# Second layer's mixer in periods of two heads with a written TensorE order: a two-layer trunk on one Trainium2 core

## The chip, the core and the metric

The kernel runs on one core of one Trainium2 chip. The time is the device time of one execution in microseconds (us), as the median of several runs. The engines are named as the profile names them: PE is TensorE's matmul stream and PEld its weight loads, DVE is VectorE, ACT is ScalarE, POOL is GpSimd, SP is the queue that issues the DMAs. PSUM is the accumulator memory that PE writes: 8 banks, each 512 fp32 values wide on 128 partitions.

A matmul of type fp32r leaves one record in the trace. A plain fp32 product leaves two, so that "x14" at the value products of the mixer stands for seven instructions; a transpose leaves one.

## The reference, cut to what matters

The program is a trunk of two layers over 512 tokens of width 1024. Each layer has a token mixer and a sparse mixture of experts; layer 0 mixes by a differential attention, layer 1 by stick-breaking attention. Only the second mixer is rewritten by the change:

```python
def stick_breaking_attention(h, w_in, w_out):
    """A[t,s] = sig(z_ts) * prod_{s<j<t} (1 - sig(z_tj)), s < t."""
    q, k, v = jnp.split(h @ w_in, 3, axis=-1)        # 16 heads of 64
    for i in range(S // Q_BLOCK):                    # 4 query blocks of 128
        q0, q1 = i * Q_BLOCK, (i + 1) * Q_BLOCK
        z = jnp.einsum('bqhd,bkhd->bhqk', q[:, q0:q1], k[:, :q1]) * scale
        log_fail = jnp.where(strict, jax.nn.log_sigmoid(-z), 0.0)
        between = lax.cumsum(log_fail, axis=-1, reverse=True) - log_fail
        a = jnp.where(strict, jnp.exp(jax.nn.log_sigmoid(z) + between), 0.0)
        outs.append(jnp.einsum('bhqk,bkhd->bqhd', a, v[:, :q1]))
    return jnp.concatenate(outs, axis=1).reshape(B, S, D) @ w_out

for i in range(DEPTH):       # h: normed, shifted and scaled by rows of cond @ ada_w[i]
    x = x + gate_1 * mixer_i(h)
    x = x + gate_2 * hierarchical_moe(h2)   # router: top-1 group, top-2 of its 8 experts
```

## The kernel before

**Arithmetic.** Activations lie transposed in SBUF, split into a high and a low fp32r part (`R_HI`, `R_LO`). Every weight piece is split likewise by `split_weights`: ACT copies the high part (L470), DVE subtracts for the low part (L471), each in two halves of 128x1024. The split pieces use two pairs of buffers in turn. A product is then three fp32r matmuls (high·high, high·low, low·high).

**Layer 1's mixer.** It runs over four groups of four heads. `qkv` makes the columns of q and k (L496 to L498, 96 matmuls of 512 columns per group) and the values (L511 to L513, 96 matmuls of 256 columns); k is brought out of PSUM by DVE (L502). `stick_group` then takes the group's two pairs of heads, and of each pair the four query blocks from the shortest (128 keys) to the longest (512 keys). For one block:

1. PE: scores of both heads (L591, fp32, 64 rows of the array each).
2. ACT: sigmoid of both heads at once (L594); POOL: causal mask by an affine select (L596); POOL: 1 − sigmoid (L599) into a second buffer, and a memset of one column (L601).
3. DVE: a scan from the last key to the first for each head (L605) into a third buffer, then the product with the sigmoid (L606).
4. PE: transposes of the 128x128 blocks (L611) into the only bank `tp`; ACT: copies out (L617).
5. PE: value products, one per block of keys and head, 128 columns each (L621); after four query blocks ACT copies the pair's result out (L624).

**What sets the order.** The PSUM tiles come from a pool by name: `mm` (2 banks), `sc` (2 times 2 banks), `tp` (1), `o` (1). The order of the instructions on each engine is set by a scheduler from the code; it puts matmuls of the next group's `qkv`, and at the end of the output product, between the scores, transposes and value products of a pair. In layer 1, chunks of the conditioning matrix (ada) for later are folded in beside it: DVE sums them in halves of 128x1024 (L322, the first of a set L319), PE turns the sum into a row (L331).

**After the mixer** the transposed result is split in eight blocks (L1185 on ACT, L1186 on DVE). `out_proj` multiplies by the output weights in two halves of columns (n = 0 and n = 1; L665 to L667, 24 matmuls for each tile of 128 tokens), adds to x with the gate (L686, L688), transposes (L692) and makes the router's logits (L699); at n = 1 the logits of n = 0 are added by L697, and routing of the tile follows, mostly on DVE. `router_prepare` makes the router's bias row (L635, L638, L640). Then the experts run (first matmul of each L1072, second L1087); their weights come through SP's queue into free slots of SBUF, in order, as slots come free (L124).

## Time and profile before

| | us |
|---|---|
| time, median of 3 runs (1639.03 to 1640.78) | 1640.48 |
| the profiled execution | 1638.01 |
| its span on the core | 1636.3 |
| PE busy | 1563.1 (96%) |
| DVE busy | 832.1 (51%) |
| ACT busy | 439.0 (27%) |
| POOL busy | 65.1 (4%) |

The span is the time from the first to the last instruction of the profiled execution. Stages overlap at their edges; the trace puts them at these times:

| stage (us from the start of the span) | from | to |
|---|---|---|
| layer 1: value products of the first group's `qkv` begin | 812.5 | |
| layer 1: first scores; last value products of the mixer | 850.0 | 1081.3 |
| layer 1: first logits of n = 1 (routing begins) | 1104.9 | |
| layer 1: first expert matmul | 1148.9 | |
| end of the span | | 1636.3 |

The busy time of an engine is a share over all stages; the start of a record and the start of the next one on the same engine tell how long it holds the engine, since the matmuls are pipelined and their records overlap.

### The profile page before, as it was taken

The numbers are of one execution on the slowest core, as the hardware profiler recorded it, in microseconds if no ns is written. First come the engines' busy times: TensorE is split into PE (matmuls) and PEld (weight loads), VectorE is DVE, ScalarE is ACT, GpSimd is POOL, SyncE is SP. The second block draws the span as 40 slices with busy tenths as digits, with TensorE's granted clock in tenths as the row PEclk, the third lists the DMA queues.
The fourth block names the chain that finished last, engine by engine and source line by source line (L and its number), as shares of the span: only waits on it lengthen the run. The fifth ranks groups of instructions, "written<-read, shape, count | busy, mean of one in ns | idle before, by whom it ended". The sixth has DMA issues, their size and how long they took to land. (4 is left out here: it accounts for less than half of the span.)

```text
span 1636.3 us, 20917 instructions
## 1 busy us (share of the span) xinstructions
PE 1563.1 (96%) x8205; PEld 920.4 (56%) x8205; DVE 832.1 (51%) x1777; ACT 439.0 (27%) x835; POOL 65.1 (4%) x120
## 2 busy tenths in 40 slices
PE   5999999899999999999799999998999999999996
PEld 2787778735454454554576675677354444544543
DVE  5888665743344244233676665547543343442435
ACT  4456555321111110110443333344211011111102
POOL 0000000000000000000003212210000000000000
PEclk9999999899999999999899999999999999999998
DMA  9886443199999999999863361331899999999994
GB/s 381 316 293 198 144 143 129 52 362 422 420 421 421 421 420 421 421 421 413 300 245 111 129 209 52 102 128 40 334 420 421 421 421 420 422 420 421 421 415 189
DMA packets 111521, 501.65 MB, mean 307 GB/s; under 512 B 14832, under 2 KB 39440, under 8 KB 65336
## 3 DMA queue, kind: packets, MB, share of 16 engines
q1 hardware_dynamic: 109688, 498.01, 76.9%
q10 hardware_dynamic: 1728, 2.23, 0.5%
q8 instruction: 68, 1.11, 0.3%
q14 instruction: 37, 0.30, 0.1%
HBM read 495.97 MB, written 4.23 MB: 306 GB/s over the span
## 5 line engine op out<-in xcount | busy, mean ns | idle before, releaser
L1072 PE MATMUL sc<-slots 128*64 128x512 f32 x2048 | 460.9, 594 | 2.7 <-DMA slots<-in_expert_w_up_dram 2.7
L1072 PEld LDWEIGHTS sc<-slots 128*64 128x64 f32 x2048 | 155.7, 137 | 301.6 <-issue 279.8
L1087 PE MATMUL sc<-slots 128*64 128x512 f32 x1024 | 226.8, 595 | 2.0 <-ACT slots L904 1.7
L895 DVE TENSOR_TENSOR slots<-slots,sc 128x512 f32<-128x512 f32 x32 | 22.0, 687 | 279.2 <-ACT slots L894 279.2
L1087 PEld LDWEIGHTS sc<-slots 128*64 128x64 f32 x1024 | 71.5, 137 | 137.1 <-issue 130.9
L908 DVE SCALAR_TENSOR_TENSOR slots<-sc,slotw,slots 128x512 f32<-128x512 f32 x64 | 45.1, 747 | 186.9 <-PE sc L1087 186.9
L927 PE MATMUL mm<-rslots 128*128 128x512 f32 x512 | 131.9, 410 | 7.4 <-DMA slots<-in_sb_w_in_dram 4.4
L927 PEld LDWEIGHTS mm<-rslots 128*128 128x128 f32 x512 | 97.2, 195 | 42.8 <-issue 21.9
L894 ACT ACTIVATE slots<-sc 128x512 f32<-128x512 f32 x32 | 19.2, 599 | 373.6 <-PE sc L1072 373.6
L917 ACT ACTIVATE rslots<-slots 128x512 fp32r<-128x512 f32 x64 | 39.9, 631 | 292.4 <-DVE slots L908 291.1
L1040 PEld LDWEIGHTS mm<-hot,rslots 128*128 128x128 f32 x896 | 109.1, 191 | 11.4 <-issue 11.4
L1040 PE MATMUL mm<-hot,rslots 128*128 128x256 f32 x896 | 114.4, 286 | 0.0
L930 DVE TENSOR_TENSOR slots<-mm,slots 128x512 f32<-128x512 f32 x144 | 95.6, 686 | 31.7 <-PE mm L927 30.0
L496 PE MATMUL mm<-rslots 128*128 128x512 f32 x256 | 104.7, 410 | 4.2 <-ACT rslots L433 3.7
L497 PE MATMUL mm<-rslots 128*128 128x512 f32 x256 | 103.9, 406 | 0.3 <-DVE rslots L434 0.3
L498 PE MATMUL mm<-rslots 128*128 128x512 f32 x256 | 104.0, 406 | 0.0
L471 DVE TENSOR_TENSOR rslots<-slots,rslots 128x1024 fp32r<-128x1024 f32 x64 | 77.9, 1228 | 44.1 <-ACT rslots L470 44.0
L322 DVE SCALAR_TENSOR_TENSOR slots<-slots,consts 128x1024 f32<-128x1024 f32 x70 | 88.6, 1290 | 6.3 <-DMA slots<-in_ada_w_dram 6.3
L470 ACT ACTIVATE rslots<-slots 128x1024 fp32r<-128x1024 f32 x64 | 66.6, 1054 | 74.2 <-PE mm L497 53.0
L511 PE MATMUL mm<-rslots 128*128 128x256 f32 x256 | 72.5, 284 | 1.5 <-ACT rslots L458 1.5
L513 PE MATMUL mm<-rslots 128*128 128x256 f32 x256 | 72.6, 284 | 0.2 <-DVE rslots L459 0.2
L512 PE MATMUL mm<-rslots 128*128 128x256 f32 x256 | 72.6, 284 | 0.0
(243 smaller groups left out, 2020.5 us busy)
## 6 DMA issues: line engine op xcount, KB each, us to landing
slots<-in_expert_w_gate_dram SPq DMA_DIRECT2D x104, 1024.0 KB, 18.8
slots<-in_expert_w_up_dram SPq DMA_DIRECT2D x104, 1024.0 KB, 15.2
slots<-in_expert_w_down_dram SPq DMA_DIRECT2D x104, 1024.0 KB, 15.7
slots<-in_ada_w_dram SPq DMA_DIRECT2D x48, 1024.0 KB, 7.4
slots<-in_expert_w_gate_dram SPq DMA_DIRECT2D x48, 512.0 KB, 6.2
slots<-in_expert_w_up_dram SPq DMA_DIRECT2D x48, 512.0 KB, 6.6
slots<-in_expert_w_down_dram SPq DMA_DIRECT2D x48, 512.0 KB, 9.1
slots<-in_diff_w_in_dram SPq DMA_DIRECT2D x12, 1024.0 KB, 5.2
```

What stands on the lines that cost most here:

```text
L322: add = dve.scalar_tensor_tensor(acc[:, c_], sl(s)[:, c_], cs[:, kb:kb + 1], acc[:, c_], op0=ALU.mult, op1=ALU.add)
L471: j = dve.tensor_tensor(rs_(ls)[:, cs_], sl(s)[:, cs_], rs_(hs)[:, cs_].bitcast(F32), op=ALU.subtract)
L496: pe.matmul(pt, lhsT=wh[:, kb, cc], rhs=rT(R_HI, kb), start=(kb == 0), stop=False)
L497: pe.matmul(pt, lhsT=wh[:, kb, cc], rhs=rT(R_LO, kb), start=False, stop=False)
L498: pe.matmul(pt, lhsT=wl[:, kb, cc], rhs=rT(R_HI, kb), start=False, stop=(kb == KB - 1))
L512: pe.matmul(po, lhsT=rT(R_HI, kb, ts), rhs=wl[:, kb, :], start=False, stop=False)
L513: pe.matmul(po, lhsT=rT(R_LO, kb, ts), rhs=wh[:, kb, :], start=False, stop=(kb == KB - 1))
L927: chain(pe.matmul(pt, lhsT=sT[:, P * i:P * i + P], rhs=parts[nn][part], start=(n + part == 0), stop=(n == len(group) - 1 and part == 1)))
L930: dve.tensor_tensor(xn, pt, xn, op=ALU.add)
L1040: chain(pe.matmul(pt[:, 256 * kk:256 * kk + 256], lhsT=rT(r, kb, slice(P * i, P * i + P)), rhs=sb[:, i, :], start=(i == 0 and r == R_HI), ...
L1072: chain(pe.matmul(pg[64 * e:64 * e + 64, w, :], lhsT=hTe[:, kb, c0:c0 + 64], rhs=sl(ws[e])[:, 512 * kk:512 * kk + 512], start=(kb == 0), s ...
L1087: chain(pe.matmul(pd[64 * e:64 * e + 64, nn, :], lhsT=hidT[:, fb, 64 * e:64 * e + 64], rhs=sl(ws[e])[:, c0:c0 + 512], start=(fb == 0), sto ...
```

## The change

**PSUM.** The pool's tiles are replaced by one tile `banks` of 8 banks; `mm`, `sc`, `tp` and `o` become fixed views of banks 0–1, 2–5, 6 and 7.

**Line.** `qkv` is cut into units: a unit of columns is 24 matmuls (one q or k block of 128 columns), a unit of values 48. `Line` holds the queue of units and splits the weights of two pieces ahead. In layer 0 six units are run before each group's mixer. In layer 1 every PE instruction of the mixer is linked to the one before it (`chain`), so that the written order holds on PE.

**Stick.** One class for the mixer of layer 1. In period n (n = 0 to 7, a pair of heads each) the order is: scores of query blocks 3 and 2; value products of pair n − 1; one unit; scores of query blocks 1 and 0; one unit; transposes of the upper blocks (14); one unit; transposes of the lower blocks (6). After the columns of a group are used up, the ten units of the output product's first half stand in the queue (`first_out`).

- 1 − sigmoid is computed by ACT as the sigmoid of the negated score (L659), so ACT does 64 sigmoids instead of 32, POOL does 64 affine selects instead of 32 and none of the 32 of L599. The last column of ones is set once.
- The scan runs in place (L674); the mask and the product stay (L675).
- Value products take two query blocks at once: 12 matmuls per pair, of 256 or 128 columns (L713), instead of 20 of 128 (the same 1280 columns for each head).
- Copies out of PSUM: two of 128x896 on ACT for the upper blocks (L699), one of 128x384 on ACT (L690) and one each of 128x256 and 128x128 on DVE (L687, L688) for the lower ones. k of layer 1 is copied by ACT.
- The bank of the second head's lower transposes is that of the pair's value result (bank 7).
- ada chunks in layer 1 are summed at two points of each period (`ada_later`), not when they are met in the queue.

**Out of order before.** `router_prepare` stands in period 6; the splits of blocks 0 to 5 in period 6, of 6 in period 7, of 7 after the last value products. x is loaded in period 7. The transposes of n = 0 use banks 4 and 5 in turn.

```diff
@@ the score step, the scan and the value products @@
-                act.activation(sg[:, :, 0:kl], pt[:, :, 0:kl], AF.Sigmoid)
...
-                pool.tensor_scalar(fb[:, :, 0:kl], sg[:, :, 0:kl], -1.0, 1.0, op0=ALU.mult, op1=ALU.add)
...
-                    dve.tensor_tensor_scan(dst, src, src, 1.0, op0=ALU.mult, op1=ALU.bypass)
...
+                act.activation(fx[:, :, at:at + kl - 1], pt[:, :, p0 + 1:p0 + kl], AF.Sigmoid, scale=-1.0)
...
+                act.activation(sg[:, :, at:at + kl], pt[:, :, p0:p0 + kl], AF.Sigmoid)
...
+                    f = fx[:, hh, at:at + kl - 1][:, ::-1]
+                    dve.tensor_tensor_scan(f, f, f, 1.0, op0=ALU.mult, op1=ALU.bypass)
...
-                for kb in range(qb + 1):
-                    for hh in range(2):
-                        pe.matmul(po[64 * hh:64 * hh + 64, P * qb:P * qb + P],
...
+            for kb, t0, aT, start, stop in steps:
+                for hh in range(2):
+                    hs = slice(64 * hh, 64 * hh + 64)
+                    chain(pe.matmul(po[hs, t0:t0 + aT[hh].shape[-1]], lhsT=v[:, kb, P * c + 64 * hh:P * c + 64 * hh + 64],
+                                    rhs=aT[hh], start=start, stop=stop))
@@ the body of layer 1 @@
-        for g in range(4):
-            q, k, v = qkv(l, g, qkv_sl, first if g == 0 else None)
-            mix(g, q, k, v, xo_sl, *rings)
...
+            line.run(4)
+            for n in range(8):
+                stick.scores(n, 0)
+                ada_later()
+                if n:
+                    stick.values(n - 1)
...
+                line.run(2 if n == 7 else 1)
...
+                stick.scores(n, 1)
+                ada_later()
+                line.run()
+                stick.transposes(0)
...
+                if n < 7:
+                    line.run()
+                stick.transposes(1, (4, 5) if n == 7 else (6, 7))
+            line.run()
+            stick.values(7)
+            split_block(xo_sl, 7)
+            line.run()
```

PE in the first group, before: scores, transposes and value products of one query block stand in between single matmuls of the next group's columns.

```order
L591 MATMUL sc<-slots 128x384
L621 MATMUL o<-slots 64x128 x5
L591 MATMUL sc<-slots 128x384
L611 MATMUL tp<-consts,slots 128x128 x4
L496 MATMUL mm<-rslots 128x512
L497 MATMUL mm<-rslots 128x512
L498 MATMUL mm<-rslots 128x512
L496 MATMUL mm<-rslots 128x512
L611 MATMUL tp<-consts,slots 128x128 x4
L621 MATMUL o<-slots 64x128
L497 MATMUL mm<-rslots 128x512
```

PE at the border of period 0 and period 1 in the changed kernel: L529 and L530 end a unit of columns, L684 are the lower transposes, L655 scores, L713 value products.

```order
L529 MATMUL banks<-rslots 128x512
L530 MATMUL banks<-rslots 128x512
L684 MATMUL banks<-consts,slots 128x128 x6
L655 MATMUL banks<-slots 128x512 x2
L655 MATMUL banks<-slots 128x384 x2
L713 MATMUL banks<-slots 64x256 x4
L713 MATMUL banks<-slots 64x128 x2
L713 MATMUL banks<-slots 64x256 x4
L713 MATMUL banks<-slots 64x128 x2
L528 MATMUL banks<-rslots 128x512
L529 MATMUL banks<-rslots 128x512
```

The score products of both heads and the value products of a whole pair now stand together, and the columns' matmuls in blocks of 24.

DVE in the second group, before: for each query block two scans and a product, with splits of weights (L471) and copies of k (L502) between them.

```order
L605 SCALAR_TENSOR_TENSOR slots<-slots 128x255 x2
L606 TENSOR_TENSOR slots<-slots 128x2x256
L605 SCALAR_TENSOR_TENSOR slots<-slots 128x383 x2
L471 TENSOR_TENSOR rslots<-slots,rslots 128x1024
L606 TENSOR_TENSOR slots<-slots 128x2x384
L605 SCALAR_TENSOR_TENSOR slots<-slots 128x511 x2
L471 TENSOR_TENSOR rslots<-slots,rslots 128x1024
L606 TENSOR_TENSOR slots<-slots 128x1024
L502 COPY slots<-mm 128x512
```

DVE at the border of period 1 and period 2 in the changed kernel: the lower scans, the splits of the next weights (L474), the copies of the lower transposes (L687, L688), the upper scans of the next pair.

```order
L674 SCALAR_TENSOR_TENSOR slots<-slots 128x255 x2
L674 SCALAR_TENSOR_TENSOR slots<-slots 128x127
L675 TENSOR_TENSOR slots<-slots 128x2x256
L674 SCALAR_TENSOR_TENSOR slots<-slots 128x127
L675 TENSOR_TENSOR slots<-slots 128x2x128
L474 TENSOR_TENSOR rslots<-slots,rslots 128x1024 x3
L687 COPY slots<-banks 128x256
L688 COPY slots<-banks 128x128
L474 TENSOR_TENSOR rslots<-slots,rslots 128x1024
L674 SCALAR_TENSOR_TENSOR slots<-slots 128x511 x2
L675 TENSOR_TENSOR slots<-slots 128x2x512
```

Two of the copies out of PSUM now stand on DVE, behind three half splits, where ACT alone did them before.

PE at the last value products, before, with the output product's matmuls (L665 to L667) around them:

```order
L611 MATMUL tp<-consts,slots 128x128 x4
L621 MATMUL o<-slots 64x128
L667 MATMUL sc<-rslots 128x512
L665 MATMUL sc<-rslots 128x512
L666 MATMUL sc<-rslots 128x512
L621 MATMUL o<-slots 64x128 x7
L667 MATMUL sc<-rslots 128x512
```

PE at the same place in the changed kernel (L742 to L744 are the output product):

```order
L744 MATMUL banks<-rslots 128x512
L713 MATMUL banks<-slots 64x256 x4
L713 MATMUL banks<-slots 64x128 x2
L713 MATMUL banks<-slots 64x256 x4
L713 MATMUL banks<-slots 64x128 x2
L742 MATMUL banks<-rslots 128x512
```

Of the 120 matmuls of the output product that come before the routing of the first tile (L697 before, L796 after), 44 stand ahead of the last value products before the change; in the changed kernel it is 75.

## Rows read from the trace of the kernel before

**Rows 1.** Windows: stretch, length, busy time of each engine, clock, DMA share, GB/s.

```profile
812.50:1081.00 268.50, 255.38 (x1493) 181.16 (x1494) 167.38 (x200) 101.08 (x174) 60.31 (x97) 0.99 0.42 144
...
1300.00:1320.00 20.00, 20.00 (x124) 12.00 (x122) 3.94 (x8) 3.38 (x6) 0.00 (x0) 1.00 1.01 422
```

**Rows 2.** Timeline of SP's queue ahead of layer 1's experts: start, length.

```profile
1099.13 52.76 SPq L124 DMA_DIRECT2D slots<-in_expert_w_down_dram  x7
```

**Rows 3.** Timeline of PE at both ends of the stretch and at the experts' start.

```profile
812.50 0.38 PE L511 MATMUL mm<-rslots 128*128 128x256 f32 x1 [1.51 <-ACT rslots L458]
...
1104.86 0.31 PE L697 MATMUL o<-logits,consts 128*128 128x40 f32 x2
...
1148.94 5.61 PE L1072 MATMUL sc<-slots 128*64 128x512 f32 x22
```

**Rows 4.** Timeline of PE: matmuls whose starts give what each kind holds.

```profile
818.20 0.28 PE L512 MATMUL mm<-rslots 128*128 128x256 f32 x1
818.32 0.28 PE L513 MATMUL mm<-rslots 128*128 128x256 f32 x1
...
849.49 0.39 PE L497 MATMUL mm<-rslots 128*128 128x512 f32 x1
849.72 0.39 PE L498 MATMUL mm<-rslots 128*128 128x512 f32 x1
850.04 0.93 PE L591 MATMUL sc<-slots 64*128 64x128 f32 x8
...
853.02 1.77 PE L591 MATMUL sc<-slots 64*128 64x384 f32 x8
857.30 0.33 PE L611 MATMUL tp<-consts,slots 128*128 128x128 f32 x1 [2.51 <-DVE slots L606]
...
892.17 0.60 PE L611 MATMUL tp<-consts,slots 128*128 128x128 f32 x4
892.70 0.43 PE L621 MATMUL o<-slots 128*64 128x128 f32 x2
...
893.95 1.09 PE L621 MATMUL o<-slots 128*64 128x128 f32 x14
894.97 0.50 PE L496 MATMUL mm<-rslots 128*128 128x512 f32 x1
```

**Rows 5.** Groups of 812 to 1105, PE only: busy, mean ns, idle before.

```profile
L699 PE MATMUL o<-wra,slots 128*128 128x40 f32 x32 | 4.1, 277 | 0.0
...
L640 PE MATMUL o<-rrow,ones_r 1*128 1x40 f32 x2 | 0.4, 288 | 0.0
```

**Rows 6.** Groups of 812 to 1082, shapes apart, columns as in Rows 5.

```profile
L322 DVE SCALAR_TENSOR_TENSOR slots<-slots,consts 128x1024 f32<-128x1024 f32 x28 | 36.0, 1302 | 0.0
L471 DVE TENSOR_TENSOR rslots<-slots,rslots 128x1024 fp32r<-128x1024 f32 x27 | 33.2, 1236 | 32.3 <-ACT rslots L470 32.3
...
L596 POOL TENSOR_SCALAR_AFFINE_SELECT slots<-slots 128x256 f32<-128x256 f32 x32 | 20.7, 647 | 163.7 <-ACT slots L594 157.5 <-DVE slots L605 3.7 <-DVE slots L322 2.5
...
L605 DVE TENSOR_TENSOR_SCAN slots<-slots 128x511 f32<-128x511 f32 x16 | 18.7, 1207 | 6.6 <-POOL slots L599 6.6
L605 DVE TENSOR_TENSOR_SCAN slots<-slots 128x383 f32<-128x383 f32 x16 | 14.4, 942 | 12.8 <-POOL slots L599 12.8
...
L606 DVE TENSOR_TENSOR slots<-slots 128x1024 f32<-128x1024 f32 x8 | 10.2, 1269 | 0.5
L606 DVE TENSOR_TENSOR slots<-slots 128x768 f32<-128x768 f32 x8 | 9.6, 1206 | 0.5
...
L594 ACT ACTIVATE slots<-sc 128x1024 f32<-128x1024 f32 x8 | 8.2, 1020 | 0.0
```

**Rows 7.** Windows of layer 1's norm and of the first scores, columns as in Rows 1.

```profile
790.00:800.00 10.00, 5.58 (x21) 3.07 (x18) 4.16 (x6) 4.43 (x5) 0.00 (x0) 0.77 0.78 276
...
850.00:860.00 10.00, 6.99 (x35) 3.81 (x34) 9.21 (x12) 4.39 (x7) 3.14 (x5) 1.00 0.61 206
```

**Rows 8.** Timeline of DVE and PE in layer 0's mixer.

```profile
70.02 2.49 DVE L322 SCALAR_TENSOR_TENSOR slots<-slots,consts 128x1024 f32<-128x1024 f32 x2
...
76.99 1.04 PE L331 MATMUL mm<-slots,ones_r 128*32 128x512 f32 x2
```

More of the change, by code (lines that the diff above doesn't have):

```diff
@@ L74, in trunk_kernel @@
     loaded = deque()
+    later = deque()
     state = {"reserve": 0}
@@ L105, in fetch, with ada_later @@
                 return s
+            later.append((s, ada))
+            if not state.get("lazy"):
+                ada_later()
+    def ada_later():
+        while later:
+            s, ada = later.popleft()
             ada_step(s, *ada)
@@ L480, in rT, with __init__, split, add @@
         return rs_(ss[kb // 4])[:, 512 * (kb % 4) + tok.start:512 * (kb % 4) + tok.stop]
-    def qkv(l, g, qkv_sl, first=None):
+    class Line:
+        def __init__(self, units, holds):
+            self.units, self.todo, self.holds = deque(), deque(), holds
+            self.left, self.w, self.open = {}, {}, 0
+            for key, unit in units:
+                self.add(key, unit)
+        def split(self, n=2):
+            while self.todo and self.open < n:
+                key = self.todo.popleft()
+                self.w[key] = split_weights(fetch(), self.holds.get(key))
+                self.open += 1
+        def add(self, key, unit):
+            if key not in self.left:
+                self.left[key] = 0
+                self.todo.append(key)
+            self.left[key] += 1
+            self.units.append((key, unit))
+        def run(self, n=1):
+            for _ in range(n):
+                self.split()
+                key, unit = self.units.popleft()
+                unit(*self.w[key])
+                self.left[key] -= 1
+                self.open -= not self.left[key]
+    def qkv_views(qkv_sl, g):
         half = slice(1024 * (g % 2), 1024 * (g % 2) + 1024)
@@ L656, in out_proj @@
         )
+        tp0 = Ring([banks[:, b, :].rearrange("p (k t) -> p k t", k=4) for b in (4, 5)])
         for n in range(2):
[L658 to L667 removed]
+            if n or not pts:
+                hl = [split_weights(fetch()) for _ in range(2)]
             if n == 1:
@@ L671, in out_proj @@
                 st["acc"] = [sc_ps(), sc_ps()]
-            else:
-                two = sc_ps()
-                pts = [mm_ps(), mm_ps(), two[:, 0, :], two[:, 1, :]]
+            elif not pts:
+                pts = [mm_ps(), mm_ps(), banks[:, 2, :], banks[:, 3, :]]
                 for i in range(NT):
-                    product(i, pts[i], 0)
+                    out_piece(pts[i], i, range(4), *hl[0])
+                rest = [lambda i=i: out_piece(pts[i], i, range(4, KB), *hl[1]) for i in range(NT)]
             for i in range(NT):
@@ L741, in route_tile @@
         pe.matmul(pr, lhsT=ident, rhs=base, start=True, stop=False)
-        pe.matmul(pr, lhsT=upper, rhs=both, start=False, stop=True)
+        ranked = pe.matmul(pr, lhsT=upper, rhs=both, start=False, stop=True)
         pos = small.tile([P, NE], F32, name="pos")
@@ L762, in route_tile @@
         if i < NT - 1:
-            pc = o_ps()[:, 0:NE]
-            pe.matmul(pc, lhsT=ones, rhs=both, start=True, stop=True)
+            pc = o_ps()[:, 128:128 + NE]
+            behind(pe.matmul(pc, lhsT=ones, rhs=both, start=True, stop=True), ranked)
             st["base"] = small.tile([P, NE], F32, name="base")
@@ L1159, in trunk_kernel @@
             reserve(4)
-        first = split_weights(fetch(), (None, diags[1]) if l else None)
+        qkv_sl = alloc(3)
+        acc_sl.extend(alloc(1))
+        reserve(0)
+        units = []
+        for g in range(4):
+            parts = part_order(l, g)
+            if l == 0:
+                order = [(part, n) for part in parts for n in range(2)]
+            elif g == 0:
+                order = ((2, 0), (2, 1), (0, 0), (1, 0), (0, 1), (1, 1))
+            else:
+                order = ((0, 0), (1, 0), (0, 1), (1, 1), (2, 0), (2, 1))
+            units.append((g, order))
+        linked.clear()
+        link = chain if l else lambda inst: inst
+        holds = {(0, 2): (None, diags[1]), (0, 0): anchor} if l else {}
+        line = Line([u for g, order in units for u in qkv_units(l, g, qkv_sl, order, link)], holds)
+        line.split(1)
         if l == 0:
```

279 lines of the change are left out of this document (177 added, 102 removed).

## Prediction, made before the changed kernel was run

> **What bounds the kernel now.** I read the windows first. In layer 1's experts PE is busy all the time and the DMA engines are full as well, at 422 GB/s [rows 1]. The second question is when this phase begins. SP's queue stands still for 52.76 us before it [rows 2]: the free slots have been filled, and the queue waits for PE to give back the first of them. So the weight stream does not set the start of the phase; PE's arrival sets the start of the stream, and the phase moves as a whole with the first expert matmul at 1148.94 [rows 3]. Before that come 44.1 us of routing from the first logits of n = 1 at 1104.86 [rows 3], which the change leaves as they are. What is left is the stretch from the first value products of `qkv` at 812.50 to 1104.86, 292.4 us. In its main part PE is busy 255.4 of 268.5 us at a clock of 0.99, DVE 167.4, ACT 101.1, POOL 60.3 [rows 1]. PE bounds it, with only 13.1 us of idle time. A change that only hid waits could win no more than these. The larger part must come from PE's own time: how long its instructions hold it.
>
> **What each kind holds.** I take the distance from start to start [rows 4]. A value product of `qkv`: 0.12 us. A product of 512 columns (columns of q and k, output product): 0.23. The last of a run before fp32 work holds 0.32, so a change of kind costs about 0.1. The scores of 384 and 512 keys of both heads stand together in one place, 7 blocks of 128 keys in 1.77 us: 0.25 per block for both heads, and 0.21 if the last matmul's own length (about 0.3) is taken off. Transposes: 0.53 us for four up to the next kind, 0.13 each, or 0.11 without the change of kind. Value products of the mixer, in the longest run there is: seven instructions, that is 3.5 blocks for both heads, in 1.02 us, 0.29 per block. Two heads side by side, as the scores show it, would give 0.21.
>
> **The sum of PE's work in the changed kernel**, same stretch:
> - value products of `qkv`: 384 × 0.12 = 46.1
> - columns of q and k: 384 × 0.23 = 88.3
> - output product, 96 of n = 0 and 24 of n = 1: 120 × 0.23 = 27.6
> - scores: 8 pairs × 10 blocks × 0.25 = 20.0 (bounds 17 and 20)
> - value products: the same 80 blocks. Pieces of 256 columns are not in the trace. I take 0.23, nearer to the scores (both are plain fp32 with the heads side by side, and all 12 stand together): 18.4 (bounds 17 and 23)
> - transposes: 160 × 0.11 = 17.2 (up to 20.8)
> - norm, ada, router and logit products, unchanged: seven groups from L699 with 4.1 to L640 with 0.4 [rows 5], together 15.9
> - changes of kind: per period three excursions into fp32 (scores with values, short scores, upper transposes; the lower ones run on into the next scores), each twice 0.1: 8 × 3 × 0.2 = 4.8
>
> Together 238.3 us. Against 292.4 that is 54.1 less: 13.1 is the idle time, and 41 is what mixing single matmuls of different kinds costs now.
>
> **What the order on PE makes of the waits.** PE now goes through a written order, so what is not ready stops all that is behind it: the next unit, and with it the copies that ACT and DVE wait to make. I follow the chain of the upper blocks. After the scores ACT needs 1.0 us for the first sigmoid, POOL 0.65 for the mask, DVE 2 × 1.21 + 1.27 + 2 × 0.94 + 1.21 = 6.8 for scans and products [rows 6]: 8.5 us. That scans in place take as long as now I assume; no row shows it. Before PE comes to the upper transposes it has the values (2.3), the short scores (0.75) and two units (2 × 5.5): 14.1 us. So 5.6 us are spare, and DVE can have four halves of split or ada ahead (1.24 and 1.30 each [rows 6]). The lower chain is shorter and has a unit and the upper transposes as cover. ACT's 32 added sigmoids cost at most 1.0 each [rows 6], 33 us over 230: ACT stays at some 60% and covers them. POOL trades 32 copies for 32 selects.
>
> The spare time goes in some places. (1) The second head's lower transposes lie in bank 7, which the value products of the same pair overwrite after 1.75 us of scores. Between them stand DVE's two copies, behind up to three half splits. If DVE is in the middle of such a half, PE waits: about 0.8 us after periods 1, 3 and 5, and 1.7 after period 2, where four ada halves stand ahead; 4.1 in all. (2) In period 6 the router's bias row needs DVE's sum, which stands behind the upper chain: 5.5 us of unit against 8.5 of chain, 3 us. (3) The transposed ada row in period 4: 1.5. Together 8.6 us (estimate; 2 if DVE meets them all early, 14 if each is doubled). 292.4 − 238.3 − 8.6 = **45.5 us** won.
>
> **Layer 0.** Its code only gets new names and fixed banks, but its order shifts: the first ada row of PE comes about 7 us earlier. DVE's sum for it ends at 72.5, PE took it at 76.99 [rows 8], so PE now waits up to 2.5 us, and at the next one perhaps 1. I take 2 (0 to 6, since a fixed ring of banks could also cost elsewhere).
>
> **The number.** 1638.0 (profiled execution) − 45.5 + 2 = 1594.5. The median of the runs is 2.5 above the profiled execution: **1597 us**. With the low bounds (values and scores 17, waits 2, switches 3, layer 0 none) it is 1582; with the high ones (values 23, transposes 20.8, waits 14, layer 0 plus 6) 1615.
>
> **Rivals.**
> A. The chain on DVE is the bound. In period 2 DVE has more to do than PE: upper chain 6.8, lower 3.5, eleven ada halves 14.3, two splits 2.5, copies 0.7, together 27.8 against about 25 of PE. Where ada and splits stand ahead of the scans in all periods, as in the first three, the wait is about 2.5 us each: 8 × 2.5 = 20 less won, 1617 us. For it speaks that the order on DVE is fixed too; against it that the later periods carry no ada sums and DVE is at 62% now.
> B. Slower than before, by the clock. In the norm of layer 1 PE was busy 5.58 of 10 us and the granted clock was 0.77 [rows 7]. If the new waits fall into every period and bring the mean granted clock over the mixer to about 0.80 (parts of it at the lower level of 1.2 GHz instead of 2.4), its 238.3 us become 298, and with 8.6 of waits and layer 0's 2 the stretch is 16 us longer than now: 1657 us. It decides from a clock of about 0.85 on, where what was won is used up. Against it: a wait of 2.51 us before 857.30 [rows 4] lies in a window with clock 1.00 [rows 7], and I expect none longer than 3. The Trainium skill (TensorE: Matmul & The Clock Gate, HAM oscillation) says that a kernel whose bursts of matmuls are parted by waits can swing between the two clock levels; it speaks against any order that makes PE wait, and this trace shows it in the norm and not in the mixer.
> C. The mixer is shorter and the end does not move, since the experts stream their weights at the DMA limit. Then the time is 1640. Against it stands the queue that waits 52.76 us for a slot [rows 2]; for it only that DMA share is 1.01 afterwards [rows 1].
> D. The change of kind is not cheaper: the 41 us of mixing are really the cost of reading fp32 operands, and the longer blocks bring back only half, 20 us, beside the idle time less the new waits (4.5). Then 1640.5 − 24.5 + 2 = 1618. Against it: 0.23 in undisturbed runs and 0.32 at a change are both in the rows. The Trainium skill (TensorEngine Tiling (Array Packing), Key Properties) says that a change of the tiling mode drains the array. By that rule only the borders of the mixer's 64-row and 64-column products would cost, and the transposes among the columns would be free; the sum would then be 1 to 2 us lower, at the same forecast.
>
> **How the numbers follow.** Forecast 0.72, A 0.12, B 0.03, C 0.03, D 0.10. Forecast and the two partial ones lie from 1582 to 1618; I take 1582 to 1619, which leaves out B and C and the tails. A measurement of this kernel can tell 0.2%, 3.3 us, from no change. Faster 0.94, same 0.03, slower 0.03.
>
> **What would show it.** In the changed trace: first routing logits about 1061 instead of 1104.86, then again 44 us to the first expert matmul; columns at 0.23 in blocks of 24; a pair's value products in 2.1 to 2.9 us; PE's waits in the mixer under 14 us, most at the value products (for DVE's copies) and the router row; clock at 0.99 there; SP's queue still waiting before the experts. If PE waits at the upper transposes in most periods, A is right; if the clock is below 0.9 in the mixer, B; if the experts' first matmul moves and the end does not, C; if the waits are small and the blocks are no faster, D.

## The result and the profile of the changed kernel

The changed kernel takes 1598.58 us (median of four runs, 1590.65 to 1603.45) against 1640.57 of the kernel before: ratio 0.9741, 95% interval 0.9698 to 0.9785. The prediction said 1597. Its profiled execution took 1601.39 us, with a span of 1599.6; the sums below are made against this one, as the prediction's were against 1638.01.

The places that [rows 3] shows of the kernel before lie here in the changed one (timeline of PE: start, length, operation; L547 first value product of layer 1's `qkv`, L796 first routing logits, L1171 first expert matmul):

```profile
820.18 0.38 PE L547 MATMUL banks<-rslots 128*128 128x256 f32 x1 [0.22 <-ACT rslots L461]
...
1066.61 0.31 PE L796 MATMUL banks<-logits,consts 128*128 128x40 f32 x2
...
1110.41 14.39 PE L1171 MATMUL banks<-slots 128*64 128x512 f32 x64
```

The stretch from the first to the second is 246.4 us, where it was 292.4; the prediction's sum was 238.3 of work and 8.6 of waits, 246.9. From the second to the third it is 43.8, where it was 44.1. But the stretch begins 7.7 us later than before, where 2 had been expected, and from the first expert matmul to the end it is 489.2 instead of 487.4. Together: −45.9 − 0.3 + 7.7 + 1.8 = −36.7 us, the difference of the two spans.

The window of the stretch and one in the experts, as in [rows 1] (busy time of PE, PEld, DVE, ACT, POOL, then clock, DMA share, GB/s):

```profile
820.18:1066.61 246.43, 239.34 (x1490) 194.23 (x1491) 178.84 (x231) 123.69 (x191) 55.63 (x70) 0.99 0.51 173
...
1300.00:1320.00 20.00, 19.76 (x93) 8.85 (x94) 11.47 (x23) 2.11 (x4) 0.00 (x0) 1.00 1.01 421
```

PE is still the bound, 239 of 246 us, with 7 us of idle time instead of 13. DVE, at 62% before, is now at 73%. The experts stream at the same rate, and SP's queue again stands before them, as in [rows 2], only for a shorter time:

```profile
1089.88 23.26 SPq L127 DMA_DIRECT2D slots<-in_expert_w_down_dram  x4
1113.23 0.38 SPq L127 DMA_DIRECT2D slots<-in_expert_w_gate_dram  x1
```

A border of two periods on PE, as written (L684 lower transposes, L655 scores, L713 value products, L528 a unit of columns). The 24 records of the value products are the 12 matmuls of a whole pair:

```profile
868.73 0.82 PE L684 MATMUL banks<-consts,slots 128*128 128x128 f32 x6
869.48 1.77 PE L655 MATMUL banks<-slots 64*128 64x512 f32 x8
871.18 2.39 PE L713 MATMUL banks<-slots 128*64 128x256 f32 x24
873.50 0.50 PE L528 MATMUL banks<-rslots 128*128 128x512 f32 x1
```

Scores hold PE for 1.70, value products for 2.32 us; the prediction had put 1.75 and 2.3.

**Where PE's time went.** For every record of PE in the stretch I took the distance to the start of the next one, less the idle time between them, and summed by kind (both columns are worked out from the two traces):

| kind | before, us | after, us | won |
|---|---|---|---|
| value products of the mixer | 34.4 | 20.2 | 14.2 |
| scores | 31.7 | 20.5 | 11.2 |
| columns of q and k | 98.6 | 89.7 | 8.9 |
| output product, 120 matmuls | 33.3 | 28.8 | 4.5 |
| transposes of the mixer | 21.2 | 17.9 | 3.3 |
| ada, router, logits, norm | 13.2 | 12.5 | 0.7 |
| value products of `qkv` | 46.9 | 49.7 | −2.8 |
| idle | 13.1 | 7.1 | 6.0 |

Together 46.0. Only 6.0 of the gain are in waits; the rest is in how long the same columns hold PE. Of the 2.8 us lost at the value products of `qkv`, 2.2 belong to the clock: in `no_waits` below, where it does not fall, they hold 47.5.

What PE still waits for in the stretch (waits: tile and line, releaser, total us, times, longest):

```profile
PE banks L731 <- DVE rrow L729: 2.6, 1, 2.6
PE banks L360 <- issue: 1.9, 1, 1.9
PE banks L360 <- DVE adab L336: 1.0, 1, 1.0
PE banks L655 <- ACT slots L534: 0.7, 1, 0.7
PE banks L549 <- DVE rslots L462: 0.5, 1, 0.5
```

The router row (L731) and the two transposed ada rows (L360) make 5.5 of 7 us. No wait stands at a value product, and one of 0.07 us at the upper transposes.

### The profile page after: what moved, and what is told of

Read it like the earlier page. It is cut to its first block, busy times and chain, and to the rows that moved or that the text cites. A ratio compares the mean times of both kernels' runs of the same rounds, so it can differ in the third digit from the quotient of the medians.

```text
span 1599.6 us, 20651 instructions
## 1 busy us (share of the span) xinstructions
PE 1531.3 (96%) x8077; PEld 911.3 (57%) x8077; DVE 833.6 (52%) x1785; ACT 451.5 (28%) x835; POOL 60.4 (4%) x92
## 5 line engine op out<-in xcount | busy, mean ns | idle before, releaser
L1171 PE MATMUL banks<-slots 128*64 128x512 f32 x2048 | 454.4, 594 | 0.0
L1171 PEld LDWEIGHTS banks<-slots 128*64 128x64 f32 x2048 | 156.2, 137 | 291.8 <-issue 277.2
L1186 PE MATMUL banks<-slots 128*64 128x512 f32 x1024 | 226.8, 595 | 1.5 <-ACT slots L1003 1.5
L1026 PE MATMUL banks<-rslots 128*128 128x512 f32 x512 | 141.6, 420 | 11.2 <-DVE slots L1029 4.6
L1186 PEld LDWEIGHTS banks<-slots 128*64 128x64 f32 x1024 | 70.7, 137 | 137.3 <-issue 130.5
L1007 DVE SCALAR_TENSOR_TENSOR slots<-banks,slotw,slots 128x512 f32<-128x512 f32 x64 | 45.1, 746 | 191.9 <-PE banks L1186 186.2
L1026 PEld LDWEIGHTS banks<-rslots 128*128 128x128 f32 x512 | 90.8, 193 | 62.7 <-DVE slots L1029 25.5
L1139 PEld LDWEIGHTS banks<-hot,rslots 128*128 128x128 f32 x896 | 109.1, 191 | 11.4 <-issue 11.4
L1139 PE MATMUL banks<-hot,rslots 128*128 128x256 f32 x896 | 114.4, 286 | 0.0
L1029 DVE TENSOR_TENSOR slots<-banks,slots 128x512 f32<-128x512 f32 x144 | 97.2, 688 | 24.8 <-PE banks L1026 24.6
L528 PE MATMUL banks<-rslots 128*128 128x512 f32 x256 | 104.4, 409 | 3.7 <-ACT rslots L436 3.7
L529 PE MATMUL banks<-rslots 128*128 128x512 f32 x256 | 102.0, 398 | 0.4 <-DVE rslots L437 0.4
L530 PE MATMUL banks<-rslots 128*128 128x512 f32 x256 | 101.8, 398 | 0.0
L474 DVE TENSOR_TENSOR rslots<-slots,rslots 128x1024 fp32r<-128x1024 f32 x64 | 77.3, 1222 | 23.6 <-ACT rslots L473 23.4
L891 ACT ACTIVATE slots<-banks,consts 128x256 f32<-128x256 f32 x64 | 35.6, 565 | 189.2 <-PE banks L1139 175.4
L547 PE MATMUL banks<-rslots 128*128 128x256 f32 x256 | 74.6, 292 | 0.2 <-ACT rslots L461 0.2
L549 PE MATMUL banks<-rslots 128*128 128x256 f32 x256 | 73.2, 286 | 0.5 <-DVE rslots L462 0.5
L548 PE MATMUL banks<-rslots 128*128 128x256 f32 x256 | 73.4, 287 | 0.2 <-DVE rslots L474 0.2
## 6 DMA issues: line engine op xcount, KB each, us to landing
slots<-in_expert_w_gate_dram SPq DMA_DIRECT2D x104, 1024.0 KB, 17.2
slots<-in_expert_w_down_dram SPq DMA_DIRECT2D x48, 512.0 KB, 10.1
```

Of the source, the lines that this page charges most:

```text
L474: j = dve.tensor_tensor(rs_(ls)[:, cs_], sl(s)[:, cs_], rs_(hs)[:, cs_].bitcast(F32), op=ALU.subtract)
L528: link(pe.matmul(pt, lhsT=wh[:, kb, :], rhs=rT(R_HI, kb), start=(kb == 0), stop=False))
L529: link(pe.matmul(pt, lhsT=wh[:, kb, :], rhs=rT(R_LO, kb), start=False, stop=False))
L530: link(pe.matmul(pt, lhsT=wl[:, kb, :], rhs=rT(R_HI, kb), start=False, stop=(kb == KB - 1)))
L547: link(pe.matmul(po, lhsT=rT(R_HI, kb, ts), rhs=wh[:, kb, :], start=(kb == 0), stop=False))
L548: link(pe.matmul(po, lhsT=rT(R_HI, kb, ts), rhs=wl[:, kb, :], start=False, stop=False))
```

## The experiments

In all of them "the stretch" is the time from layer 1's first value product to its first routing logits in the profiled execution; it moves much less from run to run than the whole time does. Its value for the changed kernel is 246.4, and 246.1 in a second profile. It does contain what TensorE's clock costs there. In the changed kernel the clock is 0.91 in two windows of 20 us (shown under `no_waits`), which is 1.8 us lost in each; in some of the edits it falls once or not at all in the stretch, and a difference of stretches has to be read with that in mind.

### The changed kernel again (after_again)

> The changed kernel once more, unedited, as the common ground of the other three. Its four runs spread from 1590.65 to 1603.45 where the kernel before spreads by 1.8. Theory: the spread is TensorE's granted clock, which falls to its lower level after short waits in some executions and not in others; then the runs again lie between 1590 and 1604, and the longer ones have the lower mean clock (about 1.6 us for each 0.001 of it). Rival: the spread is in the waits for data; then time and mean clock do not go together.

Measured: 1599.67 us (1595.95 to 1603.08, five runs; before in the same comparison 1638.31, 1635.96 to 1641.43). The five runs with their mean granted clock: 1595.95 and 1596.09 at 0.983, 1599.67 at 0.980, 1602.71 at 0.977, 1603.08 at 0.975. Time and clock go together, as the theory has it, at about 0.9 us for each 0.001 here and 1.3 in the four runs above (1590.65 at 0.985, 1603.45 at 0.975), where 1.6 was expected. That the clock makes the whole spread is not shown, since the waits of these runs are known for the profiled ones only.

### Layer 0 with one piece of weights ahead (l0_one)

```diff
-        def split(self, n=2):
+        def split(self, n=None):
+            n = n or self.ahead          # 1 in layer 0, 2 in layer 1
```

> Layer 0 splits one piece of weights ahead, as the kernel before did, instead of two; layer 1 is untouched. In the changed kernel layer 1's first value product came at 820.18 instead of 812.50, 7.7 us late, of which 5 arise at 127 to 142 us, where the scores of layer 0's second group stand in a row and the clock is at 0.50. Theory (splitting two ahead moved the ada sums and the scores in layer 0): the order of the kernel before largely comes back, the first value product comes at 813 to 815, and the time is 5 to 7 us less, about 1592. Rival (the fixed PSUM banks, or chance, made the loss): it stays at 818 to 821 and the time at 1598.

Measured: 1596.25 us (1593.63 to 1596.76), ratio 0.9736 (0.9721 to 0.9752); first value product at 815.43, stretch 246.2. The place goes where the theory put it, the time only half as far, and the theory is too simple. The layer-0 code of the changed kernel ran in eight other profiles here, and there layer 1 begins anywhere from 814.8 to 822.1. Most of the difference arises in layer 0's second group: a window there in the changed kernel, and the same in `no_waits`, whose layer 0 is the same code:

```profile
135.00:140.00 5.00, 5.00 (x11) 1.79 (x11) 2.16 (x10) 1.11 (x6) 0.00 (x0) 0.50 1.08 356
```

```profile
135.00:140.00 5.00, 5.00 (x20) 2.38 (x20) 3.88 (x22) 3.94 (x15) 0.00 (x0) 1.00 1.03 374
```

In the first the clock is 0.50, its lower level of 1.2 GHz, and PE gets through 11 records instead of 20. Ahead of it the scores of the group stand in a row with some 1.0 us of waiting for DVE, in both. It fell in five of nine profiles with this order and in none of the two with one piece ahead. From the first product of `qkv` to the first routing logits of layer 0 it takes 254.3 to 256.1 us in the five and 249.9 to 250.6 in the other four, so the fall costs about 5 us. With one piece ahead it takes 250.1 and 250.7, in the kernel before 247.1. So the order of the kernel before does not come back, against the theory; one piece ahead is as good as two where the clock does not fall. Whether it keeps the clock from falling is not shown by two profiles, nor by the spread of the runs, which is about 3 us for both kernels with one piece ahead, but also 2.5 and 3.0 for `pool_fx` and `no_filler` with two. Why the clock falls in one execution and not in the next stays open.

### The waits of layer 1 moved (no_waits), and both edits (best)

```diff
                 stick.scores(n, 1)
+                if n == 6:
+                    router = router_bias(*router)     # second matmul of the row; was ahead, in the unit
                 ada_later()
                 line.run()
+                columns_now()                         # transposes of an ada row: behind the unit
```

> In layer 1 the second matmul of the router's bias row stands one unit later, behind the short scores, and the transposes of an ada row stand behind the unit instead of in or before it. Theory (these waits are local, 2.6, 1.9 and 1.0 us, and bring two drops of the clock with them): all three waits vanish, the clock of 940 to 960 and 1000 to 1020 stays at 1.00 instead of 0.91, and the stretch from the first value product to the first routing logits is 238 instead of 246.4 us; time about 1590. Rival (the vector engine is late in any case, and the next transposes wait instead): the stretch is 243 to 246 and the time 1596 to 1598.

Measured: 1586.46 us (1583.84 to 1592.63), ratio 0.9686 (0.9662 to 0.9710). The stretch is 237.55:

```profile
814.84:1052.39 237.55, 235.15 (x1491) 191.85 (x1491) 178.97 (x231) 123.78 (x191) 56.75 (x70) 1.00 0.53 182
```

8.9 us less, of which idle time is 4.7. Most of the other 4.2 is the clock. In the changed kernel it was 0.91 in each of the two windows that hold the two longer waits, 1.8 us lost in each:

```profile
940.00:960.00 20.00, 18.06 (x116) 13.33 (x114) 13.46 (x20) 6.93 (x9) 3.00 (x4) 0.91 0.59 202
1000.00:1020.00 20.00, 17.31 (x142) 15.63 (x141) 10.88 (x16) 7.34 (x14) 6.31 (x8) 0.91 0.23 79
```

And this is how it looks behind the second of them (timeline of PE; L731 waits 2.61 us for the router row, then value products of `qkv`):

```profile
1008.07 0.41 PE L731 MATMUL banks<-rrow,ones_r 1*128 1x40 f32 x2 [2.61 <-DVE rrow L729]
...
1008.63 0.28 PE L548 MATMUL banks<-rslots 128*128 128x256 f32 x1
1008.75 0.28 PE L549 MATMUL banks<-rslots 128*128 128x256 f32 x1
...
1009.02 0.41 PE L548 MATMUL banks<-rslots 128*128 128x256 f32 x1
1009.23 0.41 PE L549 MATMUL banks<-rslots 128*128 128x256 f32 x1
```

From 1009 on each matmul holds 0.21 instead of 0.12. The theory stands: the waits were local, only one of 0.9 us at bank 7 took their place, and the two longer ones, behind which the clock fell, cost nearly twice their length.

> Both edits together: one piece ahead in layer 0 and the waits of layer 1 moved. Theory (the two losses are apart from each other): the savings add, first value product at 813 to 815, stretch 238, time about 1584. Rival (the clock gives back in one place what it loses in another): no better than the better of the two alone, about 1590.

Measured: 1586.30 us (1586.17 to 1589.32), ratio 0.9683 (0.9667 to 0.9698), stretch 237.7. The rival holds: the savings do not add in the median, and `no_waits` reaches 1583.84 in an execution, which `best` does not. Two pieces ahead are not slower in layer 0 as such: the first value product comes at 816.1 here and at 814.8 in `no_waits`. Both versions beat the changed kernel, by 12 to 13 us.

### The transposes mixed with matmuls again (mixed)

```diff
                         chain(pe.transpose(pa[:, n, :], sg[:, hh, at:at + P], ident))
+                        done += 1
+                        if done % 2 == 0 and done < 14:
+                            next(unit, None)          # three matmuls of the next unit
```

> The unit behind the upper transposes is mixed with them again: after every second of the 14 transposes come three of the unit's matmuls (periods 0 to 6). The work is the same; there are 6 more changes into fp32 and back per period, 42 in all. Theory (a change of kind and back costs 0.2 us, and mixing is what made the kernel before slow): the stretch from the first value product to the first routing logits grows by 42 x 0.2 = 8.4 us, 246.4 to 255. Rival (the kernel before was slow for other reasons, its lone score and value products): it grows by less than 2 us.

In period 6 the mixed unit belongs to the output product and here reads its operands before they are split, so that part is computed from older values. Measured: stretch 247.06, 0.6 more (1596.95 us, 1595.79 to 1604.16), with the clock at 0.91 in the same two windows as in the changed kernel. The rival holds, and one assumption of the prediction falls. The rows show why (L709 transposes, L536 columns):

```profile
880.79 0.39 PE L538 MATMUL banks<-rslots 128*128 128x512 f32 x1
881.02 0.38 PE L709 MATMUL banks<-consts,slots 128*128 128x128 f32 x2
881.15 0.48 PE L536 MATMUL banks<-rslots 128*128 128x512 f32 x1
881.47 0.40 PE L537 MATMUL banks<-rslots 128*128 128x512 f32 x1
```

The two transposes hold 0.13 us and the matmul behind them 0.32 instead of 0.23: together 0.22 for two transposes, which in a run cost 0.11 each. What looks like a price of change is the transposes' own time, shown one row later.

### The value products mixed with matmuls (v_mixed)

```diff
                     chain(pe.matmul(po[hs, t0:t0 + aT[hh].shape[-1]], ...
+                next(unit, None)                      # after each pair; periods 1 to 5
```

> In periods 1 to 5 the value products are mixed with the unit behind them: after each pair of them (both heads, one block) come three of the unit's matmuls. 5 more changes of kind per period, 25 in all; the work is the same. Mixing the transposes cost under 1 us for 42 changes. Theory (it is the products on half of the array, 64 rows or 64 columns, whose borders cost; in the kernel before a lone pair held 0.36 instead of about 0.2 and the 512-column matmul before it 0.33 instead of 0.23): 25 x 0.26 = 6.5 us more, stretch 253. Rival (changes of kind are free whatever the products): less than 1.5 us more, stretch 246 to 248.

Measured: stretch 251.68, 5.2 more (1608.09 us, 1600.20 to 1611.15). But the clock did not fall anywhere in this stretch, though the wait for the router row is 2.61 us as before (window of the stretch, and PE at that wait):

```profile
815.25:1066.93 251.68, 245.16 (x1490) 189.50 (x1491) 178.92 (x231) 124.08 (x191) 55.09 (x70) 1.00 0.50 172
```

```profile
1009.86 0.41 PE L746 MATMUL banks<-rrow,ones_r 1*128 1x40 f32 x2 [2.61 <-DVE rrow L744]
```

So 5.2 is what is left after the clock gave back some 3.6. Against `no_waits`, whose clock is 1.00 as well, PE is busy 245.2 instead of 235.2 us, and by kind (worked out as in the table above) the value products hold 4.4 us more, the columns 3.2 and the value products of `qkv` 2.5: 10.1 us, or 0.40 for each of the 25 changes. The rows of one change give 0.32 (L724 value products):

```profile
871.63 0.39 PE L538 MATMUL banks<-rslots 128*128 128x512 f32 x1
871.95 0.65 PE L724 MATMUL banks<-slots 128*64 128x256 f32 x4
872.53 0.50 PE L536 MATMUL banks<-rslots 128*128 128x512 f32 x1
872.87 0.39 PE L537 MATMUL banks<-rslots 128*128 128x512 f32 x1
```

The matmul ahead holds 0.32 instead of 0.23, a pair of 256 columns 0.58 instead of 0.46 (2.32 × 2/10 in the run of 12), and the matmul behind it 0.34 instead of 0.23; nothing is given back. The theory holds in kind, and its size of 0.26 is too small, since it left out the matmul behind; that the stretch came near the expected 253 is luck, by the clock.

A rival remains: the value products are plain fp32 with two records each, a transpose has one, so the price could be that of the plain fp32 product and not of the half array. One place in the changed kernel speaks against it. There 16 plain fp32 products of the norm, on the full array (L449, 32 records), stand among the value products of `qkv`:

```profile
823.68 0.28 PE L548 MATMUL banks<-rslots 128*128 128x256 f32 x1
823.80 3.73 PE L449 MATMUL banks<-slots 128*128 128x128 f32 x32
827.29 0.36 PE L549 MATMUL banks<-rslots 128*128 128x256 f32 x1
827.49 0.28 PE L547 MATMUL banks<-rslots 128*128 128x256 f32 x1
```

The matmul ahead holds 0.12 as always, the one behind 0.20, which is 0.08 more, and the last of the 32 records 0.03 instead of 0.11, 0.08 less: there and back costs nothing, as with the transposes. It is one place, and no run was made for it.

### The score products apart (sc_apart)

```diff
                     chain(pe.matmul(pt[:, hh, p0:p0 + kl], lhsT=q[ms, c, P * qb:P * qb + P], ...
+                    if unit:
+                        next(unit)                    # periods 0 to 5, long scores
```

> In periods 0 to 5 each of the four long score products stands alone, with three of the unit's matmuls behind it; the ada sums come just before instead of just after. Theory (two heads run side by side only when their products stand together; a lone one of 512 keys held 1.05 us in the kernel before where now both heads take 1.70 for 512 and 384 keys): 2 x 1.05 + 2 x 0.84 - 1.70 = 2.1 us, and 3 changes of kind of 0.1, so 2.4 us per period, 14 in all, stretch 260. Rival (a lone score costs no more than its half of the pair, the longer time in the kernel before was a wait): 6 x 0.3 = 2 us more, stretch 248.

Measured: stretch 259.88, 13.4 more, 2.2 per period (1610.33 us, 1610.23 to 1615.91). The clock fell once in it and not twice, so the edit itself costs some 2 us more than that. Against `no_waits` the scores alone hold 12.4 us more, 2.07 per period, where the theory had 2.1. L665 is one head's score product of 512 keys:

```profile
873.16 1.12 PE L665 MATMUL banks<-slots 64*128 64x512 f32 x2
874.22 0.50 PE L536 MATMUL banks<-rslots 128*128 128x512 f32 x1
```

Alone it holds 1.06 us. With the other head beside it both take about 0.97 (512 of the 896 columns that hold 1.70 in a period). So the second head is free only where the products stand together. The kernel before had its scores apart in part of its pairs.

### The value products in pieces of 128 columns (val128)

```diff
+            steps = [(kb, P * qb, aT, kb == 0, kb == qb) for qb, kb, aT in sorted(cut, key=lambda u: u[:2])]
```

> The value products of a pair are cut into pieces of 128 columns again, 20 matmuls instead of 12, in the order of query blocks; all else stands. Theory (two heads side by side are paid by columns): a pair's value products hold PE 2.2 to 2.5 us as now (2.3), the stretch does not move by more than 2 us. Rival (each instruction has its price, as 3.5 blocks in 1.02 us in the kernel before suggest): 2.9 us per pair, the stretch grows by 5 us.

Measured: stretch 244.73, 1.7 less (1597.87 us, 1595.11 to 1604.88). The theory holds: a pair's value products hold 2.33 us at full clock, 2.31 in pieces of 256. The 1.7 us less are no gain of the cutting: the clock fell once in this stretch and not twice (1.00 in the window 940:960, 0.91 in 1000:1020). What the change calls "values for two query blocks at once" brings no time on PE by itself. That they stand together does.

### 1 − sigmoid from GpSimd again (pool_fx)

```diff
-                act.activation(fx[:, :, at:at + kl - 1], pt[:, :, p0 + 1:p0 + kl], AF.Sigmoid, scale=-1.0)
+                pool.tensor_scalar(fx[:, :, at:at + kl - 1], sg[:, :, at + 1:at + kl], -1.0, 1.0, op0=ALU.mult, op1=ALU.add)
```

> 1 - sigmoid comes from GpSimd again (one tensor_scalar behind the mask) and not from ScalarE, as in the kernel before; the scan stays in place. It lengthens the chain from scores to upper transposes by about 1.6 us. Theory (the written order gives this chain 14.1 us and it takes about 8.5): PE does not wait for it, the stretch stays at 246.4 within 2 us. Rival (the chain is close to its cover): a wait of 1 to 2 us at the upper transposes in each period, 8 to 16 us in all.

Measured: stretch 246.94, 0.5 more (1598.78 us, 1597.87 to 1600.33). The theory holds: at the upper transposes PE does not wait. Idle time does grow by 2.2 us, and the stretch hides it, since the clock fell once and not twice. The wait is in a place that I had not named here (waits of PE; L708 are the value products, L683 the second copy of bank 7):

```profile
PE banks L708 <- DVE slots L683: 4.7, 2, 3.7
PE banks L726 <- DVE rrow L724: 3.2, 1, 3.2
```

On DVE the order around the copies had shifted with the edit: behind period 0 they stand after more ada sums, and one of these waits for its data:

```profile
869.19 1.86 DVE L325 SCALAR_TENSOR_TENSOR slots<-slots,consts 128x1024 f32<-128x1024 f32 x1 [2.12 <-DMA slots<-in_ada_w_dram]
870.98 0.41 DVE L682 COPY slots<-banks 128x256 f32<-128x256 f32 x1
871.31 0.27 DVE L683 COPY slots<-banks 128x128 f32<-128x128 f32 x1
```

PE waited 3.74 us for these copies, up to 871.64, and the clock stayed at 1.00 from 865 to 885. The chain to the upper transposes has room; the copies of bank 7 have next to none.

### No output product as filler (no_filler)

```diff
+                if n < 7:
+                    line.run()
...
-            line.run()
             stick.values(7)
             split_block(xo_sl, 7)
-            line.run()
+            line.run(6)
```

> The output product's first half is not used as filler: all its units stand behind the last value products, and periods 6 and 7 lack the three units that stood between scores and transposes. Theory (the cover is what hides the chain): in period 7 PE has 3 us of cover for a chain of 8.5 and waits 5 to 6 us at the upper transposes, 2 to 4 at the lower ones and the value products together, and 2 for the last split; the stretch grows by 9 to 12 us, and by 1 to 4 more if the clock falls. Rival (the chain is much shorter than its cover, or what is behind moves up): less than 4 us.

Measured: stretch 254.70, 8.3 more (1605.84 us, 1604.40 to 1607.35), a little under the expected 9 to 12. The main wait is where it was expected, in period 7 at the upper transposes (L698); the 2 to 4 us put at the lower ones and the value products came to 0.75:

```profile
1026.93 3.25 PE L698 MATMUL banks<-consts,slots 128*128 128x128 f32 x14 [5.97 <-DVE slots L675]
1030.93 1.51 PE L684 MATMUL banks<-consts,slots 128*128 128x128 f32 x6 [0.75 <-DVE slots L675]
```

14 transposes hold 3.25 us behind the wait, where they hold 1.45 otherwise: the clock fell here too, and is 0.50 in the windows 1027:1031 and 1031:1036.

## Why the prediction was right, and where its steps were off

**The bound and the shift.** PE bounded the stretch, the routing behind it took 44 us as before, and the experts moved as a whole; the queue that waits for slots [rows 2] was the right row for that. Rival C did not come about.

**The sum.** 246.9 predicted, 246.4 measured; so close an agreement is luck, since errors cancel. Most terms met: scores 20.0 and 20.5, value products 18.4 and 20.2 (18.5 in `no_waits`, without the clock's part), transposes 17.2 and 17.9, columns 88.3 and 89.7, output product 27.6 and 28.8. The value products of `qkv` were put at 46.1 and hold 49.7. Norm, ada, router and logits were put at 15.9, a sum of busy times; their records overlap, and what they hold PE is 12.5 (13.2 in the kernel before). The clock's part in the stretch, some 3.6 us, was not in the sum at all. Without it, in `no_waits`, PE is busy 235.2 us, against 238.3 of predicted work. (160 transposes at 0.11 make 17.6, where the sum has 17.2.)

**The price of a change.** The term of 4.8 us rested on the step from 0.23 to 0.32 before fp32 work, taken as one price for all kinds, 0.2 there and back [rows 4]. For transposes it is nothing (`mixed`), for the value products on half of the array 0.3 to 0.4 (`v_mixed`). In sum the term was about right: at full clock, in `no_waits` the columns, the value products of `qkv` and the output product hold 165.8 us, 3.8 more than their undisturbed sum of 162.0. Rival D, that the longer blocks bring back only half, fails by the table: columns and output product went to within 1.4 and 1.2 us of their undisturbed sum. The Trainium skill (TensorEngine Tiling (Array Packing), Key Properties) ties the drain to a change of the tiling mode and not of the tile. The two experiments agree with it: 0.6 us for 42 changes to full-array transposes, 10.1 for 25 changes to 64-column products.

**The waits.** 8.6 predicted, 7.1 measured, but not the same ones. The router row was put at 3 and took 2.6; the ada rows at 1.5 and took 2.9; DVE's copies of bank 7 at 4.1 and took nothing. The copies were as late as expected, only not later than PE. At the end of period 1 the three half splits and the two copies ran like this (DVE), and PE's value products started at 895.38:

```profile
891.29 3.49 DVE L474 TENSOR_TENSOR rslots<-slots,rslots 128x1024 fp32r<-128x1024 f32 x3
894.69 0.42 DVE L687 COPY slots<-banks 128x256 f32<-128x256 f32 x1
895.03 0.28 DVE L688 COPY slots<-banks 128x128 f32<-128x128 f32 x1
```

The last copy ends at 895.31, 0.07 us before PE needs it. I had put 0.8 on every such place for a DVE in the middle of a split, and the splits came in time. In `no_waits` one wait of 0.9 us at this place does appear, in `pool_fx` two with 4.7 in sum.

**The chain.** Counted from the last score product of a period to DVE's last upper product it took 7.8 to 8.2 us in periods 2 and 4 to 7, where 8.5 had been put, and 9.8, 14.6 and 9.9 in periods 0, 1 and 3, where ada sums stand ahead. In period 1 these sums themselves waited 3.24 us for their data, and the chain came 0.07 us late. Rival A, the chain on DVE as the bound, came to nothing, in period 1 by this margin; `no_filler` shows the wait that stands behind it when the cover is gone.

**Layer 0** was the mis-sized term: 2 us put (0 to 6), 7.7 measured in the profiled execution. I had looked for waits at the ada rows [rows 8]; these took the expected turn without a loss. The loss was the clock in the second group, about 5 us, which falls in some executions, and 2 to 3 us of the order in all (814.8 to 815.5 in the profiles without the fall against 812.5). The 5.7 us between 7.7 and 2 would bring the 1601.4 of the profiled execution to about 1596. That the median of 1598.58 still lies 1.6 from the predicted 1597 is luck as well: 2.5 us had been added from the profiled execution to the median, and here the median lies 2.8 below it.

**The clock.** Rival B was the right mechanism at a small size: three places, some 5 us in layer 0 and 3.6 in layer 1, and not the whole mixer. The Trainium skill (TensorE: Matmul & The Clock Gate, HAM oscillation) had spoken for it, and this trace agrees: behind waits of 1.9 and 2.6 us the clock went to its lower level. In these runs the length of a wait did not decide it: behind 2.61 us it stayed at 1.00 in `v_mixed`, behind 3.74 in `pool_fx`, and behind 1.94 in `no_filler`. The wait of 2.51 us of the kernel before [rows 4, 7], on which I had relied, did not bring it down either; one row at full clock was no proof for waits of that length. I had also read the trace of the kernel before as showing such falls in the norm and not in the mixer. It has one in the mixer, behind a wait of 1.38 us (PE, and the window behind it):

```profile
1047.73 0.34 PE L611 MATMUL tp<-consts,slots 128*128 128x128 f32 x1 [1.38 <-DVE slots L606]
```

```profile
1047.00:1052.00 5.00, 4.27 (x14) 2.41 (x14) 3.57 (x5) 1.26 (x3) 1.64 (x3) 0.66 0.62 183
```

## What to carry to other kernels

Read what an instruction holds its engine from the distances between starts, in runs and alone, and multiply: here that gave 238.3 us of PE's work against 235.2 at full clock. Do not add up busy times for it, whose records overlap. On PE keep products that use half of the array together, both halves next to each other (25 changes cost 10.1 us in `v_mixed`, heads apart 13.4 in `sc_apart`); full-array transposes may stand anywhere (0.6 us for 42 changes). Where an order is written out, list the small instructions that hang on a slow chain (a bias row, a transposed row): each stopped the whole line, and where the clock fell behind it cost nearly twice its wait. And before you take a difference of two runs for the price of an edit, compare the granted clock in both: here it hid half of one price.

## What the hardware showed that I had not expected

- A lone score product of 512 keys on 64 rows holds PE 1.06 us, two of them side by side about 0.97; cutting a value product from 256 to 128 columns costs next to nothing if the pieces stand together (2.33 us a pair against 2.31).
- The clock fell to 0.50 in layer 0 behind about 1.0 us of idle time among score products, in five of nine profiles of the same order, and did not fall behind 2.51 us in the kernel before nor behind 3.74 in `pool_fx`.
- Scans in place on DVE took 1.29 us for 511 columns instead of 1.21 [rows 6], and POOL's selects 0.99 (after the second sigmoid) instead of 0.65. The groups of the changed kernel:

```profile
L674 DVE TENSOR_TENSOR_SCAN slots<-slots 128x511 f32<-128x511 f32 x16 | 20.0, 1291 | 8.5 <-POOL slots L662 8.5
...
L668 POOL TENSOR_SCALAR_AFFINE_SELECT slots<-slots 128x256 f32<-128x256 f32 x32 | 31.5, 994 | 3.4 <-ACT slots L666 3.0 <-POOL slots L662 0.4
```

The trace shows what it goes with: not the place, but work of the other engine at the same time. Of the 16 scans of 383 columns in the changed kernel, eight have no POOL record beside them and take 0.93 us, as the ones to another buffer did (0.94 [rows 6]); the others take 0.92 to 1.16. Of the selects after the first sigmoid, the 11 with no DVE record beside them take 0.41, the others up to 1.41. In `pool_fx`, also in place, POOL's work stands beside other scans, and it is those that are long:

```profile
L669 DVE TENSOR_TENSOR_SCAN slots<-slots 128x511 f32<-128x511 f32 x16 | 23.9, 1531 | 14.5 <-POOL slots L663 14.5
L669 DVE TENSOR_TENSOR_SCAN slots<-slots 128x383 f32<-128x383 f32 x16 | 15.1, 946 | 0.0
```
